# Retention's second transposes written three half units behind the norm, and the first output weights asked for one unit sooner

## The chip, the core and the metric

The kernel runs on one core of a Trainium2 chip. The metric is the device time of one execution in microseconds (us); smaller is better. Of the core's engines these matter here: PE (TensorE: matmuls and transposes, with the weight loads PEld beside it), DVE (VectorE), ACT (ScalarE), POOL (GpSimd), and SP, whose queue issues nearly all transfers. Each engine takes its instructions in the order of its own list; between engines semaphores hold an instruction until what it needs is done.

## The reference, cut to what matters

Two batches of 512 rows and 1024 columns go through one layer. From the normed and modulated rows `h` one projection gives the inputs of two groups of heads: windowed attention (8 heads of 64) and retention (4 heads of 128, with a norm of each head's output and a gate). Their outputs stand side by side in `mix`, go through the output weights, and a gated residual add and an MLP follow.

```python
proj = h @ w_in[l]
q_a, k_a, v_a, q_r, k_r, v_r, g_r = jnp.split(proj, IN_OFFSETS, axis=-1)
o_a = windowed_attention(...)
o_r = bidirectional_retention(q_r, k_r, v_r, g_r, ...)
...
mu = jnp.mean(y, axis=-1, keepdims=True)          # the norm of one retention head
yc = y - mu
yn = yc * lax.rsqrt(jnp.mean(yc * yc, axis=-1, keepdims=True) + EPS)
return jax.nn.silu(g) * yn.reshape(B, S, RET_WIDTH)
...
x = x + g1 * (concatenate([o_a, o_r]) @ w_out[l])
```

## The kernel before

Every matrix product takes float32 operands as two parts, a rounded high part and the rest as a low part, and adds three products (high by high, high by low, low by high). So a weight block that arrives as `raw` (128 by 1024) is cast on ACT (`wh`, line 93), and DVE subtracts to get `wl` (line 101). The `raw` tiles have three buffers; on batch 1 the kept low parts of weights lie in the same three. A block that is used for both batches is written back to memory in its two parts (`kept`) and loaded from there the second time.

The work is written as **units**: one block of projection weights with its matmuls, in two half units. `run_units` loads the next unit's weights, then writes the present one's matmuls, and after each half unit it calls `between`, which moves the **stages** on by one step: generators for the attention blocks and the retention heads, which write a piece of their own work and then say with `yield n` how many half units are to pass until the next piece. So the matmuls of the units cover the chains of the stages. A scheduler then orders the instructions of each engine from priorities that follow the written order, and may move an instruction a good way if its operands are late. `hooks` are calls after a unit of a given number.

A retention head (`ret_head`, from line 405) goes: scores `prs` for four key blocks; each is scaled by the decay table `dtab` (`rsf`, DVE, line 416), cast (`rsc`, ACT, line 418) and its low part subtracted (DVE, line 419); the values go into `py`. `ryt` is `py` copied from the bank by ACT (line 436), and four transposes write `pyn` (line 440), so that rows lie on partitions. For each, DVE takes statistics (`bn`, `mv`, lines 444 and 445) and then `rva` (447); POOL raises it to the power -1/2 (`rrs`, 449); DVE makes the bias `rnb` (452); and ACT writes the normed tile `ryn` in four pieces (454). Four second transposes write `pyb` (line 459), and DVE multiplies by the gate into `mix` (460). Between `ryn` and `pyb` stands the `yield` that the change touches.

The four heads of batch 0 run while batch 1's projections `k`, `v`, `q` are written, and their ends reach into its attention. Batch 1's heads run while the projections `rq`, `rk` and `rg` of the later heads are written, and the last two end among the output units of batch 0 (`out_units(0)`). Such a unit multiplies the parts `ms` of a piece of `mix` (ACT line 760, DVE line 761) by a block `wo` of output weights into four banks `po` (lines 131, 132, 134). Background work, the modulation sums `jka_b` on DVE (line 178, one 1.28 us operation for half a loaded block), is filled in all along.

Banks: three for the units (`mm`), five for all else (`aux`): `py`, `prs`, `pyn`, `pyb`, the attention's `psc`, `ppt` and `po`, and the fourth bank of an output unit.

Of the kernel before, what the change touches and what calls it, by code (L numbers as in the profile page):

```python
# [24 lines left out]
RH, RHD = 4, 128  # L25
# [7 lines left out]
def trunk_kernel(ctx, tc, x0, x1, x0_t, x1_t, params, gate2_bias, w_ada_first, w_ada_t, w_ada_gate2, w_in_first, w_in,  # L33
# [19 lines left out]
    def aux_bank(name):  # L53
        return psum.tile([P, 512], F32, tag="aux", name=name, bufs=5)
# [4 lines left out]
    def r4f(name):  # L59
        return r4(name, F32).rearrange("p a n -> p (a n)")  # L60
# [10 lines left out]
    def f(ap):  # L71
        return ap.bitcast(F32)
# [13 lines left out]
    def raw_unit(src, name, spare=False):  # L86
        t = r4f(f"raw_{name}") if spare else work.tile([P, 1024], F32, tag="raw", name=f"raw_{name}", bufs=3)
        nc.sync.dma_start(t[:, :src.shape[1]], src)
        return t

    def split_high(t, name):
        w = [work.tile([P, 1024], F32R, tag="ws", name=f"w{s}_{name}", bufs=4) for s in "hl"]
        nc.scalar.copy(w[0], t)
        return w

    def split_unit(src, name, n):
        return split_raw(raw_unit(src, name), name, n)

    def split_raw(t, name, n):
        w = split_high(t, name)  # L100
        nc.vector.tensor_sub(w[1], t, f(w[0]))
        return [x.rearrange("p (a n) -> p a n", n=n) for x in w]
# [301 lines left out]
    def ret_head(b, h, q_, k_, v_, sg, mix):  # L404
        nm = f"{b}_{h}"
        dtab = decay_table(b, h)
        py = aux_bank(f"py_{nm}")
        sc = [None] * NT

        def scores(sb):  # L410
            ssl = slice(sb * P, (sb + 1) * P)
            psc = aux_bank(f"prs_{nm}_{sb}")
            mm3(psc, (k_[:, 0, ssl], k_[:, 1, ssl]), (q_[:, 0, :], q_[:, 1, :]), True, True)
            sf = f2(f"rsf_{nm}_{sb}")
            o = 384 - sb * P
            nc.vector.scalar_tensor_tensor(sf, psc, RHD ** -0.5, dtab[:, o:o + 512], ALU.mult, ALU.mult)
            sc[sb] = r4(f"rsc_{nm}_{sb}")
            nc.scalar.copy(sc[sb][:, 0, :], sf)
            nc.vector.tensor_sub(sc[sb][:, 1, :], sf, f(sc[sb][:, 0, :]))

        def values(sb):
            hsl = slice(h * P, (h + 1) * P)
            mm3(py, (v_[sb][:, 0, hsl], v_[sb][:, 1, hsl]), (sc[sb][:, 0, :], sc[sb][:, 1, :]), sb == 0, sb == NT - 1)

        scores(0)
        yield 1
        scores(1)
        yield 2
        for sb in range(NT):
            values(sb)  # L430
            if sb + 2 < NT:
                scores(sb + 2)
            if sb < NT - 1:
                yield 1
        yt = f2(f"ryt_{nm}")
        nc.scalar.copy(yt, py)
        yield 1
        pn = aux_bank(f"pyn_{nm}")
        for t in range(NT):
            nc.tensor.transpose(pn[:, t * P:(t + 1) * P], yt[:, t * P:(t + 1) * P], ident)  # L440
        mv = small([P, NT, 2], f"mv_{nm}")
        for t in range(NT):
            st = small([P, 6], f"bn_{nm}_{t}")
            nc.vector.bn_stats(st, pn[:, t * P:(t + 1) * P])
            nc.vector.bn_aggr(mv[:, t, :], st)
        va = small([P, NT], f"rva_{nm}")
        nc.vector.tensor_scalar(va, mv[:, :, 1], EPS, None, ALU.add)
        rs = small([P, NT], f"rrs_{nm}")
        nc.gpsimd.tensor_tensor(rs, va, neghalf[:, :NT], ALU.pow)
        yn = f2(f"ryn_{nm}")  # L450
        nb = small([P, NT], f"rnb_{nm}")
        nc.vector.scalar_tensor_tensor(nb, mv[:, :, 0], -1.0, rs, ALU.mult, ALU.mult)
        for t in range(NT):
            nc.scalar.activation(yn[:, t * P:(t + 1) * P], pn[:, t * P:(t + 1) * P], AF.Identity, bias=nb[:, t:t + 1],
                                 scale=rs[:, t:t + 1])
        yield 2
        pb = aux_bank(f"pyb_{nm}")
        for t in range(NT):
            nc.tensor.transpose(pb[:, t * P:(t + 1) * P], yn[:, t * P:(t + 1) * P], ident)
        nc.vector.scalar_tensor_tensor(mix[2 + h // 2][:, h % 2, :], pb, 0.5, sg, ALU.mult, ALU.mult)  # L460
# [61 lines left out]
    def decay_table(b, h):  # L522
        if b == 1:
            dt = mwork.tile([P, TW], F32, tag="dtab", name=f"dtab_{b}_{h}", bufs=2)
            nc.sync.dma_start(dt, kept_tables[h])
            return dt
        dt = mwork.tile([P, TW], F32, tag="dtab", name=f"dtab_{b}_{h}", bufs=2)

        nc.scalar.activation(dt, dl, AF.Copy, scale=lg[:, 0, h:h + 1])
        nc.vector.scalar_tensor_tensor(dt, dl, nlb[:, h:h + 1], dt, ALU.mult, ALU.min)  # L530
        nc.scalar.activation(dt, dt, AF.Exp)
        nc.sync.dma_start(kept_tables[h], dt)
        return dt
# [63 lines left out]
    def run_units(units, rate, hooks={}, pace=0.7):  # L597
        clock[3] = pace
        nxt = units[0].load()
        for n, u in enumerate(units):  # L600
            cur, nxt = nxt, (units[n + 1].load() if n + 1 < len(units) else None)
            if u.keep is not None:
                u.keep(cur)
            for _ in u.use(cur):
                between(rate)
            if n in hooks:
                hooks[n]()
# [53 lines left out]
    one = {}  # L661
# [48 lines left out]
    def out_units(b, late=None):  # L710
# [35 lines left out]
        def unit(hf, kq):  # L746
            hs = slice(hf * 512, (hf + 1) * 512)

            key = f"wo{hf}_{kq}"

            def load():
                if b == 1:
                    w = kept_unit(key, f"wo{b}_{hf}_{kq}", 512, (late, "ws2", 3))
                else:
                    w = split_unit(w_out[hf, kq], f"wo{b}_{hf}_{kq}", 512)
                if hf == 0:
                    ms = halves[kq] = []
                    for k in range(2):
                        m_ = r4(f"ms_{b}_{kq}_{k}")
                        nc.scalar.copy(m_[:, 0, :], mix[kq][:, k, :])  # L760
                        nc.vector.tensor_sub(m_[:, 1, :], mix[kq][:, k, :], f(m_[:, 0, :]))
                        ms.append(m_)
                if kq == 2:
                    gr[hf] = gate_row(0, b, hs)
                return w, halves[kq]

            def use(wm):
                w, ms = wm
                if kq == 0:
                    banks[hf] = [(mm_bank if t < 3 else aux_bank)(f"po_{b}_{hf}_{t}") for t in range(NT)]  # L770
                for ts_ in ((0,), (1,), (2,), (3,)) if kq == 3 else ((0, 1), (2, 3)):
                    mm3_late([(banks[hf][t], [ms[k][:, i, t * P:(t + 1) * P] for i in range(2)],
                               (w[0][:, k, :], w[1][:, k, :]), kq + k == 0, kq + k == 4) for t in ts_ for k in range(2)], 1)
                    if ts_[-1] == 1:
                        yield
                if kq == 3:
                    for t in range(NT):
                        if hf == 0:
                            x2[t] = x2_tile(t)
                            tc.keep_in_program_order(nc.sync.dma_start(x2[t], xin[b][t * P:(t + 1) * P, :]))  # L780
                        g_ = f2(f"go_{b}_{hf}_{t}")
                        nc.vector.tensor_tensor(g_, banks[hf][t], gr[hf], ALU.mult)
                        nc.vector.tensor_tensor(x2[t][:, hs], x2[t][:, hs], g_, ALU.add)
                        if hf == 1 and b == 1:
                            store(t)
                            squares(hf, t)
                            if t > 0:
                                scaled(t - 1)
                    if hf == 0:
                        later.append((clock[0] + 2, lambda: [squares(hf, t) for t in range(NT)]))  # L790
                    elif b == 1:
                        scaled(NT - 1)
                yield
            return Unit(load, use, None, (lambda wm: keep_unit(key, wm[0])) if b == 0 else None)

        def norm2():
# [399 lines left out]
    units = first_v  # L1196
    for h in range(RH):
        units = units + ret_units(hT[0], 0, h)
    run_units(units, 1.3, {7: lambda: extra.append(norm_x1())})
    units = attn_units(hT[1], 1) + ret_v_units(hT[1], 1)  # L1200
    for h in range(RH):
        units += ret_units(hT[1], 1, h)
    run_units(units, 1.3)
    units, norm2_0 = out_units(0)
    run_units(units, 1.0)
    flush()
# [5 lines left out]
    units, norm2_1 = out_units(1, late)  # L1212
# [367 lines left out]
```

## Time and profile before

| what | value |
|---|---|
| median of 3 runs | 1106.5 us (1105.95 to 1106.68) |
| the profiled execution | 1105.71 us, its span 1103.9 us |
| mean granted clock of TensorE | 0.998 |
| busy share of the span: PE, PEld, DVE, ACT, POOL | 98%, 81%, 78%, 47%, 4% |
| 196 to 247 us (51.0): PE busy, DVE busy | 48.48, 40.90 us |
| 364 to 378 us (14.0): PE busy, DVE busy | 12.87, 9.85 us |

A line of the profile in order of time gives the start, the time taken, the engine, the line of the kernel and the operation, the tile written and those read (without buffer numbers), and in brackets how long the engine stood before it and for whom. A matmul's time overlaps that of the next, so for PE the distance from start to start is what counts: 0.227 us for 512 columns. A list of waits gives the waiting engine with its tile, the one waited for, the sum in us, the number of times and the longest.

### The profile page before, as it was taken

The page shows a single profiled execution, that of the slowest core. Times are in us where ns is not written, and L with a number is a line of the kernel's source. Part 1 is how long each engine was busy: PE and PEld are TensorE (multiplying, and loading weights), DVE is VectorE, ACT ScalarE, POOL GpSimd, SP SyncE. Part 2 cuts the span into 40 slices and gives each one's busy share as a digit, 9 for nine tenths or more (in the row PEclk, how much of TensorE's full clock was granted, in tenths as well). Part 3 has the DMA queues.
Part 4 walks back from the last instruction along what each step waited for, and adds up shares of the span by engine and source line. Part 5 has one row for each costly group of instructions (what it writes and reads, how often), then busy time and mean ns, then how long its engine had stood idle before and what let it go on. Part 6 is the DMA issues. An engine that isn't in the chain of part 4 may idle for free.

```text
span 1103.9 us, 14022 instructions
## 1 busy us (share of the span) xinstructions
PE 1078.9 (98%) x5021; PEld 888.9 (81%) x5021; DVE 864.6 (78%) x1448; ACT 515.9 (47%) x885; POOL 49.0 (4%) x55
## 2 busy tenths in 40 slices
PE   7999999999999999999999999999999999999997
PEld 5777788778888788888888888888788888888886
DVE  7979989877887787889878777886659754589786
ACT  6576666545653433574333343333443733335342
POOL 1000000000000001000000000000000000002213
PEclk9999999999999999999999999999999999999999
DMA  9889698765545698734546444452883556525504
GB/s 374 334 301 322 248 379 289 234 194 176 181 139 191 233 360 300 274 123 139 189 169 198 155 162 166 169 181 105 307 322 106 187 194 203 198 77 191 191 19 153
DMA packets 86746, 232.73 MB, mean 211 GB/s; under 512 B 8578, under 2 KB 20882, under 8 KB 86676
## 3 DMA queue, kind: packets, MB, share of 16 engines
q1 hardware_dynamic: 86084, 231.25, 60.2%
q8 instruction: 39, 0.64, 0.2%
q10 hardware_dynamic: 432, 0.57, 0.1%
q14 instruction: 31, 0.25, 0.1%
q0 software_dynamic: 160, 0.02, 0.0%
HBM read 160.75 MB, written 71.06 MB: 210 GB/s over the span
## 4 chain that ended last, share of the span: by engine, by line
PE 87%; DVE 8%; ACT 2%; DMA 1%; issue 1%; POOL 0%; POOLq 0%; ACTq 0%; DVEq 0%
PE x L1350 16%; PE px_None L933 15%; PE y L1350 12%; PE py_None L933 11%; PE po L132 3%; PE po L134 3%; PE po L131 3%; PE po L393 2%; PE ppt L386 2%; PE psc L360 1%; PE pj_rq L131 1%; PE pj_rq L132 1%; PE pj_rq L134 1%; PE pj_rg L134 1%; PE pj_rk L132 1%; PE pj_rk L131 1%
## 5 line engine op out<-in xcount | busy, mean ns | idle before, releaser
L1290 DVE TENSOR_TENSOR uc_l<-ur,uc_h 128x1024 fp32r<-128x1024 f32 x56 | 68.4, 1221 | 53.1 <-ACT uc_h L1290 36.0
L1350 PE MATMUL x<-wc_h,uc_h 128*128 128x512 f32 (+1 forms) x264 | 100.9, 383 | 0.7 <-ACT adacc L246 0.7
L1350 PE MATMUL x<-wc_l,uc_h 128*128 128x512 f32 (+1 forms) x264 | 101.0, 383 | 0.0
L1350 PE MATMUL x<-wc_h,uc_l 128*128 128x512 f32 (+1 forms) x264 | 101.0, 383 | 0.0
L1290 ACT CAST uc_h<-ur 128x1024 fp32r<-128x1024 f32 x56 | 58.9, 1051 | 77.3 <-PE x L1350 25.1
L1350 PE MATMUL y<-wc_h,uc_h 128*128 128x512 f32 x192 | 74.7, 389 | 0.0
L1350 PE MATMUL y<-wc_l,uc_h 128*128 128x512 f32 x192 | 74.7, 389 | 0.0
L1350 PE MATMUL y<-wc_h,uc_l 128*128 128x512 f32 x192 | 74.7, 389 | 0.0
L1290 ACT CAST wc_h<-w 128x1024 fp32r<-128x1024 f32 x48 | 50.5, 1051 | 48.1 <-PE x L1350 24.7
L1290 DVE TENSOR_TENSOR wc_l<-w,wc_h 128x1024 fp32r<-128x1024 f32 x48 | 58.6, 1220 | 17.6 <-ACT wc_h L1290 13.8
L1350 PEld LDWEIGHTS x<-wc_h,uc_h 128*128 128x128 f32 x264 | 49.6, 188 | 10.9 <-ACT adacc L246 1.2
L1350 PEld LDWEIGHTS x<-wc_h,uc_l 128*128 128x128 f32 x264 | 49.6, 188 | 9.8
L1350 PEld LDWEIGHTS x<-wc_l,uc_h 128*128 128x128 f32 x264 | 49.6, 188 | 9.6
L131 PE MATMUL po<-wh_wo,ms 128*128 128x512 f32 x128 | 50.2, 396 | 0.0
L132 PE MATMUL po<-wh_wo,ms 128*128 128x512 f32 x128 | 49.8, 392 | 0.1
L178 DVE CUSTOM_DVE_ANT_0 jka_b<-raw_adat,cb,cols 128x1024 bf16<-128x1024 f32 x38 | 48.2, 1279 | 0.1
L838 ACT CAST wc_s4h<-raw_w 128x1024 fp32r<-128x1024 f32 x16 | 16.8, 1052 | 63.1 <-PE px_None L933 54.1
L370 ACT ACTIVATE st<-st,negm 128x256 f32<-128x256 f32 (+1 forms) x64 | 35.2, 554 | 15.6 <-DVE negm L365 15.6
L1350 PEld LDWEIGHTS y<-wc_h,uc_l 128*128 128x128 f32 x192 | 36.0, 188 | 7.5
L1350 PEld LDWEIGHTS y<-wc_h,uc_h 128*128 128x128 f32 x192 | 36.0, 188 | 7.5
L1350 PEld LDWEIGHTS y<-wc_l,uc_h 128*128 128x128 f32 x192 | 36.0, 188 | 7.5
L933 PE MATMUL py_None<-hch,wc_a 128*128 128x512 f32 x120 | 39.7, 389 | 0.0
(378 smaller groups left out, 2954.8 us busy)
## 6 DMA issues: line engine op xcount, KB each, us to landing
ur<-spill SPq DMA_DIRECT2D x56, 512.0 KB, 4.5
raw_adat<-in_w_ada_t_dram SPq DMA_DIRECT2D x36, 512.0 KB, 6.9
raw_w<-in_w_mlp_dram SPq DMA_DIRECT2D x32, 512.0 KB, 3.5
spill<-s SPq DMA_DIRECT2D x64, 256.0 KB, 3.7
w<-in_w_mlp_dram SPq DMA_DIRECT2D x32, 512.0 KB, 5.2
spill<-u SPq DMA_DIRECT2D x48, 256.0 KB, 2.0
raw_ada<-in_w_ada_t_dram SPq DMA_DIRECT2D x12, 512.0 KB, 9.3
x<-in_x_dram SPq DMA_DIRECT2D x12, 512.0 KB, 7.2
```

What stands on the lines that cost most here:

```text
L131: nc.tensor.matmul(ps, lhs[0], rhs[0], start=start, stop=False)
L132: nc.tensor.matmul(ps, lhs[late], rhs[1 - late], start=False, stop=False)
L134: nc.tensor.matmul(ps, lhs[1 - late], rhs[late], start=False, stop=stop)
L178: nc.vector.tensor_tensor_reduce(junk(f"jka_{name}_{sec}_{kc}_{b}"), t, cb[:, b, :], 1.0, bcol[:, sec * KC + kc:sec * KC + kc + 1] if bias ...
L360: nc.tensor.matmul(psc[:, :w], qs[hh][:, isl], k_[:, s, j0 * P:j1 * P], start=(s == 0), stop=(s == 1))
L370: nc.scalar.activation(st[hh][:, :w], st[hh][:, :w], AF.Exp, bias=negm[:, hh:hh + 1], scale=0.125, accum_out=den[:, hh:hh + 1])
L386: nc.tensor.transpose(pt[:, hh * P:(hh + 1) * P], st[hh][:, jj * P:(jj + 1) * P], ident)
L393: nc.tensor.matmul(po, va[:, j0 + jj, g].rearrange("p s e -> p (s e)"), pts[jj][:, s, :], start=(jj == 0 and s == 0), stop=(jj == nj - 1 a ...
L838: nc.scalar.copy(hi, src)
L933: self.last = nc.tensor.matmul(bank[:, cs], x[:, k, :], y, start=first and k == 0 and i == 0, stop=last and k == 3 and i == 2, skip_group_ ...
L1290: last_split[:] = [nc.scalar.copy(hi, src), nc.vector.tensor_sub(lo, src, f(hi))]
L1350: nc.tensor.matmul(out, left[n][x][:, i, ts_], right[n][y][:, i, cs], start=first and i == 0 and k == 0, stop=end and i == 1 and k == 2, s ...
```

## The change

Two edits. The first writes the second transposes of all four heads of batch 0 and of heads 0 and 1 of batch 1 three half units behind the norm, not two; for heads 2 and 3 of batch 1 it stays two. The second asks for the raw block of the first output weights in a hook behind the unit `len(units) - 2` of the list before (the units of batch 1), and `out_units` takes it from there, where it had asked for it itself when its first unit was loaded.

```diff
@@ -453,7 +453,7 @@
         for t in range(NT):
             nc.scalar.activation(yn[:, t * P:(t + 1) * P], pn[:, t * P:(t + 1) * P], AF.Identity, bias=nb[:, t:t + 1],
                                  scale=rs[:, t:t + 1])
-        yield 2
+        yield 3 if b == 0 or h < RH - 2 else 2
         pb = aux_bank(f"pyb_{nm}")
         for t in range(NT):
             nc.tensor.transpose(pb[:, t * P:(t + 1) * P], yn[:, t * P:(t + 1) * P], ident)
@@ -752,7 +752,8 @@
                 if b == 1:
                     w = kept_unit(key, f"wo{b}_{hf}_{kq}", 512, (late, "ws2", 3))
                 else:
-                    w = split_unit(w_out[hf, kq], f"wo{b}_{hf}_{kq}", 512)
+                    t = one.pop((key, b), None) or raw_unit(w_out[hf, kq], f"wo{b}_{hf}_{kq}")
+                    w = split_raw(t, f"wo{b}_{hf}_{kq}", 512)
                 if hf == 0:
                     ms = halves[kq] = []
                     for k in range(2):
@@ -1200,7 +1201,7 @@
     units = attn_units(hT[1], 1) + ret_v_units(hT[1], 1)
     for h in range(RH):
         units += ret_units(hT[1], 1, h)
-    run_units(units, 1.3)
+    run_units(units, 1.3, {len(units) - 2: lambda: one.update({("wo0_0", 0): raw_unit(w_out[0, 0], "wo0_0_0")})})
     units, norm2_0 = out_units(0)
     run_units(units, 1.0)
     flush()
```

How the built lists differ at the places that the prediction speaks of. In these rows the number after the operation's tile is the head (`py_2`), the head and key block (`prs_2_1`, `rsc_2_1`), or for `po_0_3` the half and the row block; the last number only tells buffers apart; `x4` is four in a row.

PE, where batch 0's output units begin, behind the second transposes of batch 1's head 1. Before:

```order
L459 MATMUL pyb_1_3861<-ident,ryn_1_3799 128x128 x4
L124 MATMUL py_2_3808<-rsc_2_0_3815,rv_0_2861 128x512
L125 MATMUL py_2_3808<-rsc_2_0_3815,rv_0_2861 128x512
L126 MATMUL py_2_3808<-rsc_2_0_3815,rv_0_2861 128x512
L124 MATMUL prs_2_2_3917<-rq_2_3527,rk_2_3598 128x512
L125 MATMUL prs_2_2_3917<-rq_2_3527,rk_2_3598 128x512
L126 MATMUL prs_2_2_3917<-rq_2_3527,rk_2_3598 128x512
L124 MATMUL py_2_3808<-rsc_2_1_3839,rv_1_2870 128x512
L131 MATMUL po_0_0_3898<-wh_wo_0_0_3873,ms_0_0_3877 128x512
```

Now:

```order
L459 MATMUL pyb_1_3908<-ident,ryn_1_3799 128x128 x4
L124 MATMUL prs_3_0_3917<-rq_3_3722,rk_3_3774 128x512
L125 MATMUL prs_3_0_3917<-rq_3_3722,rk_3_3774 128x512
L126 MATMUL prs_3_0_3917<-rq_3_3722,rk_3_3774 128x512
L131 MATMUL po_0_0_3892<-wh_wo_0_0_3867,ms_0_0_3871 128x512
L131 MATMUL po_0_1_3893<-wh_wo_0_0_3867,ms_0_0_3871 128x512
L131 MATMUL po_0_2_3894<-wh_wo_0_0_3867,ms_0_0_3871 128x512
L131 MATMUL po_0_3_3895<-wh_wo_0_0_3867,ms_0_0_3871 128x512
L124 MATMUL py_2_3825<-rsc_2_0_3832,rv_0_2847 128x512
```

Head 3's first scores have come up behind `pyb_1`; the first `po` stands four matmuls nearer to it, and head 2's `py` and second half of scores behind the `po`.

DVE at the same place, from head 1's `rnb` to the low parts `ms`. Before:

```order
L452 SCALAR_TENSOR_TENSOR rnb_1_3800<-mv_1_3782,rrs_1_3797 128x4
L416 SCALAR_TENSOR_TENSOR rsf_2_0_3813<-prs_2_0_3809,dtab_2_3806 128x512
L419 TENSOR_TENSOR rsc_2_0_3815<-rsf_2_0_3813,rsc_2_0_3815 128x512
L178 ISA jka_b_2_1_3831,mod_s_90<-raw_adat_3648,cb,cols 128x1024
L178 ISA mod_s_90 128x1
L416 SCALAR_TENSOR_TENSOR rsf_2_1_3837<-prs_2_1_3833,dtab_2_3806 128x512
L344 SCALAR_TENSOR_TENSOR rg_3_3854<-rg_3_3854,pj_rg_3_3818 128x512
L178 ISA jka_b_3_0_3859,mod_s_90<-raw_adat_3753,cb,cols 128x1024
```

Now:

```order
L452 SCALAR_TENSOR_TENSOR rnb_1_3800<-mv_1_3782,rrs_1_3797 128x4
L178 ISA jka_b_2_1_3821,mod_s_90<-raw_adat_3648,cb,cols 128x1024
L178 ISA mod_s_90 128x1
L416 SCALAR_TENSOR_TENSOR rsf_2_0_3830<-prs_2_0_3826,dtab_2_3823 128x512
L419 TENSOR_TENSOR rsc_2_0_3832<-rsf_2_0_3830,rsc_2_0_3832 128x512
L101 TENSOR_TENSOR wl_wo_0_1_3880<-raw_wo_0_1_3877,wh_wo_0_1_3879 128x1024
L344 SCALAR_TENSOR_TENSOR rg_3_3847<-rg_3_3847,pj_rg_3_3808 128x512
L178 ISA jka_b_3_0_3852,mod_s_90<-raw_adat_3747,cb,cols 128x1024
L178 ISA mod_s_90 128x1
L416 SCALAR_TENSOR_TENSOR rsf_2_1_3858<-prs_2_1_3854,dtab_2_3823 128x512
```

The second `rsf` of head 2 has gone behind the low half of the second output weights, the gate and one more `jka_b`.

The queue of transfers, round the first output weights. Before:

```order
L119 DMA wl_rg_3_3738<-kept_in_2037 128x1024
L525 DMA dtab_3_4079<-kept_t_101 128x896
L88 DMA raw_wo_0_0_3871<-in_w_out_dram 128x1024
L88 DMA raw_adat_3753<-in_w_ada_t_dram 128x1024
L110 DMA kept_wo_0_3895<-wh_wo_0_0_3873 128x1024
L88 DMA raw_wo_0_1_3883<-in_w_out_dram 128x1024
```

Now:

```order
L119 DMA wl_rg_3_3732<-kept_in_2037 128x1024
L525 DMA dtab_3_3914<-kept_t_101 128x896
L88 DMA raw_wo_0_0_3806<-in_w_out_dram 128x1024
L88 DMA raw_adat_3747<-in_w_ada_t_dram 128x1024
L110 DMA kept_wo_0_3889<-wh_wo_0_0_3867 128x1024
L88 DMA raw_wo_0_1_3877<-in_w_out_dram 128x1024
```

Nothing has changed place on this queue; the load of `raw_wo_0_0` still waits for a buffer that the last matmuls of the projection `rq` of head 3 free.

Of batch 0's heads: in PE's list `pyb` of head 1 stands at row 795 and that of head 2 at row 901 in both, with `pyn` of head 1 six matmuls earlier now; between `pyn` and `pyb` of head 3 stand 15 rows before and 43 now, the added ones being projection matmuls and the first attention block's transposes and values.

## The prediction

> **What bounds the kernel now.** I read the page first, then the list of waits on the matrix engine, then the lines in order of time round each wait.
>
> ```profile
> span 1103.9 us, 14022 instructions
> PE 1078.9 (98%) x5021; PEld 888.9 (81%) x5021; DVE 864.6 (78%) x1448; ACT 515.9 (47%) x885; POOL 49.0 (4%) x55
> ```
>
> PE is busy in 98% of the span, so only time in which PE stands still can be won, and every new wait of PE adds to the end. Over 182 to 490 us, the stretch from the retention of batch 0 to the first output units, the list of PE's waits is short:
>
> ```profile
> PE pyb L459 <- ACT ryn L454: 2.5, 2, 1.3
> PE px L268 <- ACT x L742: 1.5, 1, 1.5
> PE py L124 <- ACT rsc L418: 1.0, 1, 1.0
> ```
>
> The `pyb` waits are what the first edit speaks of: the second transposes come before the normed tile `ryn` is there. The `py` wait stands in the first output unit, which the second edit speaks of; `px` comes later and keeps its cause. To price a stall I take the time from one matmul's start to the next and subtract 0.227 us, the step of 512-column matmuls back to back. Head 1, head 2 and head 3 of batch 0, in order of time:
>
> ```profile
> 200.42 0.17 DVE L447 TENSOR_SCALAR rva<-mv 128x4 f32<-128x4 f32 x1
> 200.73 1.01 POOL L449 TENSOR_TENSOR rrs<-rva,neghalf 128x4 f32<-128x4 f32 x1 [18.78 <-DVE rva L447]
> 200.97 0.39 PE L131 MATMUL pj_v<-h,wh_v 128*128 128x512 f32 x1
> 201.77 0.16 DVE L452 SCALAR_TENSOR_TENSOR rnb<-mv,rrs 128x4 f32<-128x4 f32 x1 [1.18 <-POOL rrs L449]
> 201.97 1.16 ACT L454 ACTIVATE ryn<-pyn,rnb,rrs 128x128 f32<-128x128 f32 x3 [2.28 <-DVE rnb L452]
> 202.48 0.33 PE L459 MATMUL pyb<-ident,ryn 128*128 128x128 f32 x1 [1.12 <-ACT ryn L454]
> ...
> 224.28 0.17 DVE L447 TENSOR_SCALAR rva<-mv 128x4 f32<-128x4 f32 x1
> 225.20 1.28 DVE L178 CUSTOM_DVE_ANT_0 jka_b<-raw_adat,cb,cols 128x1024 bf16<-128x1024 f32 x1
> 226.41 0.16 DVE L452 SCALAR_TENSOR_TENSOR rnb<-mv,rrs 128x4 f32<-128x4 f32 x1
> 226.67 1.51 ACT L454 ACTIVATE ryn<-pyn,rnb,rrs 128x128 f32<-128x128 f32 x4 [2.49 <-DVE rnb L452]
> 226.73 0.39 PE L134 MATMUL pj_q<-h,wl_q 128*128 128x512 f32 x1
> 227.18 0.33 PE L459 MATMUL pyb<-ident,ryn 128*128 128x128 f32 x1
> 227.27 0.48 PE L124 MATMUL prs<-rq,rk 128*128 128x512 f32 x1
> 227.59 0.27 PE L459 MATMUL pyb<-ident,ryn 128*128 128x128 f32 x1
> ...
> 242.89 0.39 PE L131 MATMUL pj_rv<-wh_rv,h 128*128 128x512 f32 x1
> 244.62 0.30 PE L459 MATMUL pyb<-ident,ryn 128*128 128x128 f32 x1 [1.34 <-ACT ryn L454]
> ```
>
> Head 1 loses 202.48 - 200.97 - 0.227 = 1.28 us, head 2 227.18 - 226.73 - 0.227 = 0.22, head 3 244.62 - 242.89 - 0.227 = 1.50: together 3.0 us. The chain in front is `pyn`, four statistics on DVE, `rva`, the power on POOL (1.01 us), `rnb`, then four `ryn` that start 0.35 us apart. A matmul that follows a lone transpose takes 227.59 - 227.27 = 0.32 us to the next start, 0.09 more than the usual step; the four transposes of heads 2 and 3 stand scattered among matmuls, which costs about 3 x 0.09 more for each of the two heads than one block would, 0.5 us together.
>
> The place where the output units begin, batch 1's head 1 (`rnb`, `ryn`), head 2 (`rsf`, `rsc`, `py`) and the first unit's `ms` and `po`:
>
> ```profile
> 357.23 0.33 SPq L88 DMA_DIRECT2D raw_wo<-in_w_out_dram  x1
> 361.20 1.05 ACT L93 CAST wh_wo<-raw_wo 128x1024 fp32r<-128x1024 f32 x1 [3.38 <-DMA raw_wo<-in_w_out_dram]
> 362.28 1.22 DVE L101 TENSOR_TENSOR wl_wo<-raw_wo,wh_wo 128x1024 fp32r<-128x1024 f32 x1 [0.91 <-ACT wh_wo L93]
> 363.53 0.33 SPq L88 DMA_DIRECT2D raw_wo<-in_w_out_dram  x1
> 367.43 0.16 DVE L452 SCALAR_TENSOR_TENSOR rnb<-mv,rrs 128x4 f32<-128x4 f32 x1 [1.12 <-POOL rrs L449]
> 367.94 1.05 ACT L93 CAST wh_wo<-raw_wo 128x1024 fp32r<-128x1024 f32 x1 [3.53 <-DMA raw_wo<-in_w_out_dram]
> 368.90 1.50 ACT L454 ACTIVATE ryn<-pyn,rnb,rrs 128x128 f32<-128x128 f32 x4
> 370.94 0.69 DVE L419 TENSOR_TENSOR rsc<-rsf,rsc 128x512 fp32r<-128x512 f32 x1 [2.73 <-ACT rsc L418]
> 371.28 0.48 PE L124 MATMUL py<-rsc,rv 128*128 128x512 f32 x1
> 371.54 1.28 DVE L178 CUSTOM_DVE_ANT_0 jka_b<-raw_adat,cb,cols 128x1024 bf16<-128x1024 f32 x1
> 372.75 0.69 DVE L416 SCALAR_TENSOR_TENSOR rsf<-prs,dtab 128x512 f32<-128x512 f32 x1
> 373.47 0.62 ACT L418 CAST rsc<-rsf 128x512 fp32r<-128x512 f32 x1 [1.15 <-DVE rsf L416]
> 373.99 2.18 ACT L760 CAST ms<-mix 128x512 fp32r<-128x512 f32 x4
> 374.14 0.50 PE L124 MATMUL py<-rsc,rv 128*128 128x512 f32 x1 [1.03 <-ACT rsc L418]
> 374.66 1.19 PE L131 MATMUL po<-wh_wo,ms 128*128 128x512 f32 x4
> 377.09 0.51 PE L132 MATMUL po<-wh_wo,ms 128*128 128x512 f32 x1
> ```
>
> The weights' first cast waits 3.38 us for its load, the second 3.53; ACT takes its work in order, so `ryn` and `rsc` of the retention queue behind it, DVE then stands 2.73 us, and PE pays at the end: from 371.28 to 377.09 it goes 16 matmuls further, which is 16 x 0.227 = 3.6 us of work in 5.8 us, thus 2.2 us of stalls.
>
> **The change part by part.** It adds and removes no arithmetic. Both edits alter only when code is written out, and the built order says how far that carries.
>
> *The second transposes, heads of batch 0.* Head 1: `pyb` stays at row 795 of PE's list; `pyn` comes 6 matmuls sooner (6 x 0.227 = 1.4 us), but the table operation of head 3, which stood ahead of the chain on DVE, now stands inside it:
>
> ```profile
> L530 DVE SCALAR_TENSOR_TENSOR dtab<-dl,nlb,dtab x4: 1143/1146/1147, 51.4 to 194.1; 128x896 f32<-128x896 f32 x4
> ```
>
> 1.4 sooner less 1.15 for it leaves about 0.2: the stall goes from 1.28 to 1.1. Head 2: `pyb` stays at row 901, now as one block of four, so that all four `ryn` are needed. On DVE a `qs` and a `jka_b` (0.7 + 1.2) stand among its statistics where `rsc` and `qs` (0.6 + 0.7) stood, so `rva` comes about 0.6 later, at 224.85, but no `jka_b` stands ahead of `rnb` any more: by head 1's steps (0.31 and 1.04) `rnb` is there at 226.2, not 226.41. The first `ryn` follows 0.2 later, the fourth starts 3 x 0.35 behind that and ends after another 0.45, at 227.9; PE wants the fourth transpose at 226.73 + 0.227 + 3 x 0.11 = 227.29. That is 0.6 lost, and 0.25 more because `rsc` of head 3 now queues behind the block of `ryn`: 0.85 against 0.22. Head 3: between `pyn` and `pyb` stand 43 rows instead of 15, so its 1.50 goes. In exchange the first attention block's scores come earlier; following DVE and ACT through them, PE waits about 0.2 for the fourth `ryn` (a score takes the bank of `pyn`) and 0.3 for `mix` behind two `jka_b`. After: 1.1 + 0.85 + 0.5 = 2.45; before 3.0, and the 0.5 of scattered transposes. **About -1.0 us**; bounds -3.5 (no wait left at all, 3.0 + 0.5) and +1 (head 2 and the new waits twice as long, and head 1 as before).
>
> *Heads of batch 1, first output unit.* No `pyb` of batch 1 shows a wait, so there is nothing to win by holding them back; but head 3's scores move from some 95 instructions behind to just behind head 1's `pyb`, and DVE's order changes. From `rnb` (367.43): `jka_b` comes first (to 368.7), then `rsf` (to 369.3), `rsc`, and then, ahead of head 2's second `rsf`, the low half `wl_wo` of the second weights (1.22), the gate `rg` (0.6) and the next `jka_b` (1.2). The first weights are requested when the last matmul of `rq` for head 3 has freed a buffer; in the new order three matmuls of `py` stand behind that one instead of ahead, so each weight step is 0.7 sooner, the second cast at 367.26, `rsc` on DVE at 370.25. Then 370.25 + 0.6 + 1.14 + 0.6 + 1.2 = 373.8 for that `rsf`, against 372.75: 1.05 later. The casts `ms` stand behind its `rsc` on ACT, so PE's first `po` can start at 375.7, where it was 374.66. PE now has only head 3's three score matmuls (371.3 to 372.05) to run in front of it and waits 3.6 us. The low parts of `ms` then come in time. Against 2.2 before: **+1.4 us**. Bounds: -0.5 (`wl_wo` and `rg` find DVE idle after all, 1.9 us sooner) and +3.5 (a later landing, below).
>
> *The weights asked for sooner.* In the transfer queue's list nothing changes place: head 3's table load at row 183, `raw_wo` at 184, a background load, and the second `raw_wo` at 187, in both. Worth 0 by itself, apart from the 0.7 above; what would hide a longer landing is nothing, since ACT waits there already.
>
> *Later.* Heads 2 and 3 now share the output units. Following the same chain for head 3: `pyb` has 24 matmuls (5.5 us) behind `pyn`, the chain on DVE carries three extra `ms` differences (0.6 each), about 0.2 us of wait. **+0.2**, 0 to 1.
>
> Sum: 1105.7 (the profiled execution: span 1103.9 and 1.8 around it) - 1.0 + 1.4 + 0.2 = 1106.3. The median shown, 1106.5, is 0.8 above that execution, so I forecast **1107.1**.
>
> The transfer deserves a check against the Trainium skill. From issue (363.53) to the cast (367.94) the second weights took 4.4 us. "DMA: Bandwidth & Descriptors" (the section with the two cost components) gives about 2.0 us fixed plus bytes over 436 GB/s, so 3.2 us for these 512 KB, as an estimate; the trace disagrees. By the page, `ryn` would be set by `rnb`, the chain would run 0.5 sooner, and the sum would be 0.5 lower; the row decides here.
>
> **The rivals.** *The waits simply vanish* (chance 0.22). For it: head 3's cover grows to nearly three times its length, and `pyn` of head 1 comes 1.4 us sooner. Against it: heads 1 and 2 get no more matmuls between. Price: the 3.0 and the 0.5 won and nothing lost in the first output unit, 1106.5 - 3.5 = 1103.0.
>
> *The second weights land late* (0.18), the slower side. The landing times of these loads:
>
> ```profile
> DMA to landing us min/median/max: 3.6/5.0/6.1
> ```
>
> Here the two took 4.0 (357.23 to 361.20) and 4.4 us to their casts, and the second is asked for only when `wl_wo` has read the first. At 6.1 the second slips by 1.7, both together by 3.8, and `ryn`, `rsc`, `wl_wo` and `ms` with them, since nothing is left for PE in front of `po`: 1108.8 to 1110.9, of which I take 1109.8. It decides once the two take 1.6 us longer in sum than here. For it: ACT already stands idle at both casts, so there is no slack. Against it: the queue's order round them is the same.
>
> *The clock drops* (0.05).
>
> ```profile
> PEclk9999999999999999999999999999999999999999
> ```
>
> The granted clock stays at 9 tenths or more in all slices, and PE's longest wait in this stretch is 1.5 us; one of 3.6 us would be new. If the matmuls behind it ran at half rate for as long as it lasted, half of 3.6 us would be lost: 1108.9. "TensorE: Matmul & The Clock Gate" of the Trainium skill (Part 1) says that the clock is halved after an idle window of about 3.4 us, and that the window runs freely, so that a wait of this size seldom fills one; no run here shows it yet.
>
> *The change does not do what it says* (0.10): the scheduler puts the work back, heads 1 and 2 as shown, and all is as before, 1106.5.
>
> **How the numbers follow.** The forecast, waits traded one for another, has 0.45; of it 0.07 lies above 1108.7 and 0.03 below 1104.3. A difference under 0.2% (2.2 us) cannot be told from none in this kernel. Faster: 0.22 + 0.03 = 0.25. Slower: 0.18 + 0.07 and half of the 0.05, less a little for landings that are only somewhat late, 0.25. Same: the rest, 0.50. The forecast's own range is 1105.0 to 1109.0; to leave out no more than two tenths it reaches to 1103.3 and 1109.8.
>
> **What would show it.** Right: no wait at head 3's `pyb` in batch 0 and still about one at head 1's; four `pyb` of head 2 in one block behind a wait; in the first output unit the wait at `po` for `ms` where it was at `py` for `rsc`, 3 us or more, with `wl_wo` ahead of the second `rsf` on DVE. Wrong: head 1's wait gone, or that `po` wait under 2 us (then faster); or PE waits for a `raw_wo` landing, or matmuls at twice 0.227 us (then slower).

## The result

The changed kernel took 1112.2 us (median of 6 runs, 1111.7 to 1112.6), the kernel before 1106.6 us in the same comparison (1105.9 to 1107.0): a ratio of 1.0053, with an interval of 1.0042 to 1.0063. So the change costs 5.6 us; the forecast was 1107.1 with a range up to 1109.8. One matmul wait of 4.7 us and a spell of halved clock behind it make most of it. The same order of instructions, built once more and timed again (below), cost 4.7 us, so the size is known to about 1 us.

### The profile after

The page of the changed kernel: span, PE's busy time, and the granted clock in 40 slices.

```profile
span 1110.4 us, 14018 instructions
PE 1082.3 (97%) x5021; PEld 891.5 (80%) x5021; DVE 866.0 (78%) x1448; ACT 515.9 (46%) x885; POOL 49.9 (4%) x55
PEclk9999999999999899999999999999999999999999
```

PE does the same 5021 matmuls and is *busy* for 3.4 us longer; one clock slice shows an 8. PE's waits from 182 to 490 us:

```profile
PE po L131 <- ACT ms L761: 4.7, 1, 4.7
PE pyb L459 <- ACT ryn L454: 0.9, 2, 0.7
PE py L934 <- ACT wc_a L839: 0.7, 1, 0.7
PE po L131 <- DVE go L783: 0.3, 1, 0.3
PE py L124 <- ACT rsc L418: 0.2, 1, 0.2
```

The `pyb` waits shrank from 2.5 to 0.9 us as meant, and the longest wait of the whole stretch is new: the first output matmul waits for `ms`. The wait for `wc_a` is the same in the kernel before (0.7 us), and the `px` wait has not gone: it is 1.6 us and now stands just behind 490 us. To see where the time came from, take places in PE's list up to which both kernels have done the same matmuls. Two of them, before:

```profile
360.23 0.39 PE L124 MATMUL py<-rsc,rv 128*128 128x512 f32 x1
...
395.18 0.39 PE L131 MATMUL po<-wh_wo,ms 128*128 128x512 f32 x1
```

and after:

```profile
360.54 0.48 PE L124 MATMUL py<-rsc,rv 128*128 128x512 f32 x1
...
400.60 0.48 PE L131 MATMUL po<-wh_wo,ms 128*128 128x512 f32 x1
```

Up to 360 us, thus over all of batch 0's heads, the change costs 360.54 - 360.23 = 0.3 us; over the stretch from there to 395 us, which holds the first output units, 400.60 - 395.18 - 0.3 = 5.1; over the rest 6.5 (the spans) - 5.4 = 1.1. The first output unit in order of time, after:

```profile
356.97 0.33 SPq L88 DMA_DIRECT2D raw_wo<-in_w_out_dram  x1
362.11 1.05 ACT L93 CAST wh_wo<-raw_wo 128x1024 fp32r<-128x1024 f32 x1 [4.54 <-DMA raw_adat<-in_w_ada_t_dram]
...
368.89 1.05 ACT L93 CAST wh_wo<-raw_wo 128x1024 fp32r<-128x1024 f32 x1 [4.03 <-DMA raw_wo<-in_w_out_dram]
369.85 1.49 ACT L454 ACTIVATE ryn<-pyn,rnb,rrs 128x128 f32<-128x128 f32 x4
371.88 0.69 DVE L419 TENSOR_TENSOR rsc<-rsf,rsc 128x512 fp32r<-128x512 f32 x1 [2.04 <-ACT rsc L418]
372.25 0.40 PE L126 MATMUL prs<-rq,rk 128*128 128x512 f32 x1
372.49 1.22 DVE L101 TENSOR_TENSOR wl_wo<-raw_wo,wh_wo 128x1024 fp32r<-128x1024 f32 x1
373.63 0.68 DVE L344 SCALAR_TENSOR_TENSOR rg<-rg,pj_rg 128x512 f32<-128x512 f32 x1
374.23 1.28 DVE L178 CUSTOM_DVE_ANT_0 jka_b<-raw_adat,cb,cols 128x1024 bf16<-128x1024 f32 x1
375.43 0.68 DVE L416 SCALAR_TENSOR_TENSOR rsf<-prs,dtab 128x512 f32<-128x512 f32 x1
376.15 0.62 ACT L418 CAST rsc<-rsf 128x512 fp32r<-128x512 f32 x1 [3.80 <-DVE rsf L416]
376.67 2.17 ACT L761 CAST ms<-mix 128x512 fp32r<-128x512 f32 x4
377.34 2.08 PE L131 MATMUL po<-wh_wo,ms 128*128 128x512 f32 x4 [4.69 <-ACT ms L761]
```

The order on DVE is the one forecast: `wl_wo`, `rg`, `jka_b`, and only then head 2's second `rsf`, `rsc`, `ms`. It begins later than forecast: the first weights were requested 0.4 us later than reckoned and took 5.1 us from request to cast (before: 4.0), so the second cast came at 368.89 where 367.26 had been reckoned. (The profile puts the end of that first wait down to the background load requested 0.4 us behind the weights; in four other kernels with the same gap to the load ahead it names `raw_wo`, after 4.8 to 5.0 us.) PE goes 372.25 to 377.34 between two matmuls, 4.86 us more than a step of 0.227. And the four `po` then take 2.08 us, where they took 1.19. The same place by time stretches (the number ahead of the last two is the granted clock):

```profile
375.00:376.00 1.00, 0.00 (x0) 0.00 (x0) 1.00 (x3) 0.00 (x0) 0.00 (x0) 0.80 1.04 426
376.00:377.00 1.00, 0.00 (x0) 0.00 (x0) 1.00 (x3) 0.85 (x2) 0.00 (x0) 0.50 1.04 410
...
381.00:382.00 1.00, 1.00 (x4) 0.81 (x3) 1.00 (x1) 0.00 (x0) 0.00 (x0) 0.50 0.00 0
382.00:383.00 1.00, 1.00 (x5) 0.79 (x5) 0.12 (x2) 0.00 (x0) 0.00 (x0) 0.79 0.00 0
```

The clock is at half from 375.6 to 382.4. PE works from 377.34, so by estimate half of 382.4 - 377.34 is lost, 2.5 us. Together: 4.86 - 2.2 (the stalls before) + 2.5 = 5.2, against 5.1 by the fixed places.

### The profile page after: what moved, and what is told of

It is laid out like the page before. It is cut to its first block, busy times and chain, and to the rows that moved or that the text cites. A ratio compares the mean times of both kernels' runs of the same rounds, so it can differ in the third digit from the quotient of the medians.

```text
span 1110.4 us, 14018 instructions
## 1 busy us (share of the span) xinstructions
PE 1082.3 (97%) x5021; PEld 891.5 (80%) x5021; DVE 866.0 (78%) x1448; ACT 515.9 (46%) x885; POOL 49.9 (4%) x55
## 4 chain that ended last, share of the span: by engine, by line
PE 86%; DVE 9%; ACT 2%; issue 1%; DMA 1%; POOL 1%; POOLq 0%; DVEq 0%; ACTq 0%
PE x L1351 16%; PE px_None L934 15%; PE y L1351 12%; PE py_None L934 11%; PE po L131 3%; PE po L132 2%; PE po L134 2%; PE po L393 2%; PE ppt L386 2%; PE psc L360 2%; DVE jka_b L178 1%; PE pj_rq L131 1%; PE pj_rq L132 1%; PE pj_rq L134 1%; PE pj_rk L132 1%; PE pj_rk L131 1%
```

## The experiments

All times are medians, beside a median of the kernel before on the same chip.

### Which edit, and which heads

**Batch 0's heads alone.**

```diff
-        yield 2
+        yield 3 if b == 0 else 2
```

> Later second transposes for the four heads of batch 0 alone; batch 1's heads and the weight request as before. Theory A (the longer last heads of batch 0 push every later stage on by half a unit, so that in batch 1 head 3's scores fall in front of the first output unit): PE waits about 4.7 us at the first output matmul for the first ms, the matmuls behind it run at half clock, 1111 to 1112.5 us. Rival B (as the prediction put it: the heads of batch 1 that are held back make the new order): no such wait, about 1106.8 us (batch 0's own balance, +0.3).

Measured: 1110.9 us (before 1106.0), ratio 1.0047 [1.0032, 1.0062], 0.1 us under the range expected. The longest of its waits of PE:

```profile
PE po L131 <- ACT ms L760: 4.8, 1, 4.8
```

Theory A holds: batch 0's heads alone make the wait in batch 1.

**Batch 1's heads 0 and 1 alone.**

```diff
-        yield 2
+        yield 3 if b == 1 and h < RH - 2 else 2
```

> Later second transposes for heads 0 and 1 of batch 1 alone. Theory A: the first output unit stays as before, no wait over 2 us at its first matmul, 1106 to 1107 us. Rival B: the 4.7 us wait and the half clock are here, 1111 us or more.

Measured: 1105.6 us (before 1106.0), ratio 0.9995 [0.9986, 1.0005]. Its three longest waits are those of before:

```profile
PE pyb L459 <- ACT ryn L454: 2.5, 2, 1.3
PE px L268 <- ACT x L742: 1.4, 1, 1.4
PE py L124 <- ACT rsc L418: 0.9, 1, 0.9
```

Rival B, which is how the prediction told it, falls: the edited heads of batch 1 do neither harm nor good.

**One head: head 3 of batch 0.**

```diff
-        yield 2
+        yield 3 if b == 0 and h == 3 else 2
```

> The later second transposes for one head alone, head 3 of batch 0. Theory A (one half unit more at the end of batch 0's stages is enough to shift all later stages): the wait at the first output matmul stands as in the whole change, 4 to 5 us, with the half clock behind it; the wait at head 3's transposes (1.34 us) is gone: 1110 to 1111.5 us. Rival B (the shift needs the heads of batch 1, or all four of batch 0): the gain alone, 1105 us.

Measured: 1111.0 us (before 1105.6), ratio 1.0052 [1.0035, 1.0069]; the two longest waits of PE:

```profile
PE po L131 <- ACT ms L760: 3.7, 1, 3.7
PE pyb L459 <- ACT ryn L454: 1.1, 1, 1.1
```

One half unit at the end of batch 0 costs as much as the whole change, though the wait is 3.7 us where 4 to 5 were expected; the clock was at half for 6.8 us here. The kernel keeps only two stages going at a time, so a head that ends later lets every later stage start later. PE's built order at the first output matmul, before, ends with head 2's own matmuls:

```
pyb_1 x4 | py_2 (rsc_2_0) x3 | prs_2_2 x3 | py_2 (rsc_2_1) x1 | po_0_0 ...
```

and with this one edit, 130 us after the edited place, it reads:

```
prs_2_1 x3 | pyb_1 x4 | prs_3_0 x3 | po_0_0 ...
```

Head 2 is four of its `py` matmuls and a score block further back, and PE has only head 3's three `prs` in hand while the chain of head 2's `rsf` and `rsc`, which `ms` queues behind, is still open.

**The first edit without the sooner request.**

```diff
-    run_units(units, 1.3, {len(units) - 2: lambda: one.update({("wo0_0", 0): raw_unit(...)})})
+    run_units(units, 1.3)
```

> The first edit alone, for all six heads; the weights are asked for where the kernel before asks. On every engine and in the transfer queue the instructions stand in the same order as in the whole change, so theory A says: the same time as the whole change, 1111 to 1112.5 us. Rival (the sooner request does something by itself): 1 us or more away from that.

Measured: 1110.7 us (before 1106.1), ratio 1.0040 [1.0025, 1.0056]; that is 0.3 us under the range expected and overlaps the whole change's interval. The orders are the same instruction for instruction on PE, DVE, ScalarE and the transfer queue, so the second edit changes nothing.

### The late landing

**First try: spare tiles, requested one unit sooner.**

```diff
-    {len(units) - 2: lambda: one.update({("wo0_0", 0): raw_unit(w_out[0, 0], "wo0_0_0")})}
+    {len(units) - 3: lambda: one.update({("wo0_0", 0): raw_unit(w_out[0, 0], "wo0_0_0", True),
+                                         ("wo0_1", 0): raw_unit(w_out[0, 1], "wo0_0_1", True)})}
```

> The changed kernel with the first two output weights loaded into spare tiles one unit sooner, so that neither cast waits for a load; PE's and DVE's orders are the same. Theory A (order and late loads add up): ryn and rsc of head 2 start about 1.5 us sooner, the wait at the first output matmul falls from 4.7 to about 3.2 us; 1110.7 us if the clock still drops, 1108.3 us if it stays. Rival (the order on DVE alone makes the wait, loads don't matter): 1112.2 us.

Measured: 1110.3 us (before 1106.0), ratio 1.0043 [1.0026, 1.0060]; the wait at `po` is 4.6 us. The trace says why this decides nothing:

```profile
354.56 0.32 SPq L525 DMA_DIRECT2D dtab<-kept_t  x1
356.19 1.28 SPq L88 DMA_DIRECT2D raw_wo<-in_w_out_dram  x3
...
362.54 1.05 ACT L93 CAST wh_wo<-raw_wo 128x1024 fp32r<-128x1024 f32 x1 [1.17 <-DMA raw_wo<-in_w_out_dram]
```

The requests stood behind the decay table in the transfer queue, left together, and the first took 6.3 us to its cast: no sooner than before. The second cast, at 363.81 in this trace, no longer stood in front of `ryn`, but the late first one held `wl_wo` on DVE, and head 1's statistics behind it.

**Second try: requested ahead of the decay table.**

```diff
-    {len(units) - 3: ...
+    {len(units) - 5: ...
```

> The changed kernel with the first two output weights in spare tiles and asked for ahead of head 3's decay table in the transfer queue, so that they land before ScalarE comes to their casts. PE's order is the same; on DVE the second weights' low half and two statistics stand a few places earlier. If late landings made the part of the wait that was not forecast (4.9 where 3.6 us were): the second cast no longer stands in front of ryn, rsc of head 2 is ready at 370.5, the wait at the first output matmul falls to 3.4 to 3.7 us and the first output matmul starts 1.2 us sooner. Rival (DVE's order sets the wait, and something else takes the place of the landings): the wait stays at 4.5 us or more. In either case it stays over 3 us, since rg and jka_b still stand ahead of rsf; time 1109 to 1111 us.

Measured: 1110.2 us (7 runs, 1108.3 to 1111.7; before 1106.3), ratio 1.0035 [1.0023, 1.0047]. ScalarE and PE in order of time:

```profile
351.13 1.05 ACT L93 CAST wh_wo<-raw_wo 128x1024 fp32r<-128x1024 f32 x1 [3.16 <-DMA raw_wo<-in_w_out_dram]
...
363.71 1.05 ACT L93 CAST wh_wo<-raw_wo 128x1024 fp32r<-128x1024 f32 x1 [0.26 <-PE pj_rk L132]
...
368.50 1.51 ACT L454 ACTIVATE ryn<-pyn,rnb,rrs 128x128 f32<-128x128 f32 x4 [3.26 <-DVE rnb L452]
376.37 2.07 PE L131 MATMUL po<-wh_wo,ms 128*128 128x512 f32 x4 [3.37 <-ACT ms L761]
```

The first cast still waits for its load, but 11 us sooner than in the changed kernel; the second, at 363.71, waits for none, and `ryn` starts right behind `rnb`. The wait is 3.4 us, at the lower end of the 3.4 to 3.7 expected. So the late landing made some 1.3 of the 4.7 us, and what stays is the chain on DVE (`wl_wo`, `rg` and `jka_b` still run ahead of the second `rsf`). The time is 3.9 us above the kernel before, where the change cost 4.7 to 5.6; that is about what the shorter wait gives, but the intervals overlap. In this execution the clock was still halved (375.0 to 381.8). Of the seven runs of this one program, two had a mean granted clock of 0.998 and took 1108.3 and 1108.5 us; those at 0.995 took 1110.2 to 1111.7.

### The halved clock

Idle matmuls behind head 3's first `prs`, into a bank that is overwritten later; n = 11, 13 and 6. With 11 and 6 the order of everything else is unchanged; with 13 five rows of PE's list behind the first output matmuls change place.

```diff
             mm3(psc, (k_[:, 0, ssl], k_[:, 1, ssl]), (q_[:, 0, :], q_[:, 1, :]), True, True)
+            if (b, h, sb) == (1, 3, 0):
+                for _ in range(n):
+                    nc.tensor.matmul(py, k_[:, 0, ssl], q_[:, 0, :], start=True, stop=True, ...)
```

> The changed kernel with 11 idle matmuls (11 x 0.227 = 2.5 us, into a bank that is overwritten) between head 3's scores and the first output matmul, where PE waits 4.7 us; the order of all else is the same. If the half clock behind the wait is due to PE's standing still: the wait shrinks to about 2.2 us, the granted clock stays at 1.00 from 372 to 384, and the time falls by the 2.5 us that the slow matmuls cost, to 1109.7 us. Rival (the clock drops for another reason, such as the time or the work behind): the idle matmuls hide in the wait, nothing changes, 1112.2 us.

Measured with 11: 1109.9 us (10 runs, 1107.4 to 1113.8; before 1106.0), ratio 1.0039 [1.0028, 1.0050]. Its median is the expected one, and its mechanism is not:

```profile
376.00:378.00 2.00, 0.79 (x3) 0.67 (x4) 2.00 (x4) 1.98 (x4) 0.00 (x0) 1.00 0.90 365
378.00:380.00 2.00, 2.00 (x6) 1.51 (x5) 2.00 (x4) 1.25 (x3) 0.00 (x0) 0.54 0.05 12
380.00:382.00 2.00, 2.00 (x7) 1.59 (x6) 2.00 (x4) 0.00 (x0) 0.00 (x0) 0.61 0.00 0
```

The wait was 1.92 us, and the clock still went to half, from 378.2 to 381.6, beginning 0.9 us *after* PE had started again. So a short wait can be enough, and it isn't its length alone that counts. That gave theory C, which the next two were to test.

> As with 11 idle matmuls, but 13, so that about 1.5 us of standing still is left in front of the first output matmul. Theory C (the clock is judged in windows of 3.41 us that run freely, and halved for the next window when PE was busy in less than about half of one): 1.5 us can leave no window under 55% busy, so the clock is never halved there; every run at 1110 us or less, median about 1108.7 us, and a spread like that of the kernel before (2.7 us). Rival (any wait of over about 1.4 us can halve it, or the cause is not PE's standing still): runs up to 1112 us or more, as with 11.

Measured with 13: 1110.9 us (5 runs, 1109.6 to 1112.4; before 1106.1), ratio 1.0044 [1.0031, 1.0056].

```profile
377.16 1.20 PE L131 MATMUL po<-wh_wo,ms 128*128 128x512 f32 x4 [1.51 <-ACT ms L764]
...
378.00:380.00 2.00, 2.00 (x10) 1.60 (x9) 2.00 (x4) 1.20 (x3) 0.00 (x0) 1.00 0.04 10
380.00:382.00 2.00, 2.00 (x10) 1.62 (x10) 1.95 (x4) 0.00 (x0) 0.00 (x0) 1.00 0.00 0
...
398.11 0.48 PE L131 MATMUL po<-wh_wo,ms 128*128 128x512 f32 x1
```

In the profiled execution the clock stayed at 1.00. The place that the changed kernel reached at 400.60 comes at 398.11 here, 2.5 us sooner (the idle matmuls left out of the count); the first output matmul began 0.2 us sooner, so the halved clock had cost about 2.3 us there. But the expectation on the runs fails, and they look as the rival has it: of the other four one took 1109.8 us with a mean clock of 0.998, three took 1110.9 to 1112.4 with 0.995 or 0.996. Where the clock fell in those, whether the wait was longer or another one did it, stays open, since only one execution was profiled; the `px` wait near 489 us, 2.2 us in that one, is a candidate.

> As with 11 idle matmuls, but 6, so that about 3.3 us of standing still is left. Theory C: wherever the windows of 3.41 us fall, one of them has over 1.65 us of it, so the clock is always halved for one or two windows: median about 1110.8 us, no run under 1109 us. Rival (only a wait longer than a whole window of 3.4 us halves it): the clock stays, 1109 us or less.

Measured with 6: 1110.2 us (4 runs, 1108.5 to 1111.3; before 1106.1), ratio 1.0036 [1.0023, 1.0050]; wait 3.0 us, clock at half from 377.1 to 380.5. That speaks against the rival in the profiled execution; one run of 1108.5 us at a clock of 0.998 lies under the bound of theory C, so "always" is not borne out.

### The wait taken away

`ms` is split from batch 0's `mix`, which is complete long before. Splitting it four units sooner takes it out of the queue behind `rsc`:

```diff
-                if hf == 0:
-                    ms = halves[kq] = [] ...   # the two splits
+                if hf == 0 and kq not in halves:
+                    split_mix(kq)
...
+    units_0, norm2_0 = out_units(0)
+    run_units(units, 1.3, {..., len(units) - 4: lambda: [norm2_0.split_mix(q) for q in (0,)]})
```

On the changed kernel:

> The changed kernel with the first unit's two ms split four units sooner (their source, batch 0's mix, is complete long before), so that the first output matmuls wait neither for rsf and rsc of head 2 nor for the weights. If the queue of ms behind rsc on ScalarE is what sets the wait: no wait over 1.5 us between 370 and 385, granted clock 1.00, 4.9 + 2.5 us less: 1105 us. Rival (PE then only waits at the next thing, head 2's py or the second unit's ms): a wait of 3 us or more there, 1109 us or more.

Measured: 1104.4 us (before 1105.6), ratio 0.9987 [0.9978, 0.9996].

```profile
PE px L268 <- ACT x L750: 1.3, 1, 1.3
...
372.00:377.00 5.00, 5.00 (x25) 4.13 (x24) 4.91 (x8) 1.20 (x3) 0.00 (x0) 1.00 0.97 359
```

The wait is gone (the longest that is left in this stretch is the `px` wait), PE is busy without a break from 372 to 377, the clock stays, and nothing takes the wait's place. So the wait for `ms`, with the halved clock behind it, is what the change lost. Two further kernels have the sooner split without the change, and with batch 0's part alone:

> The kernel before with the first unit's two ms split four units sooner. Theory A: of its 2.2 us of stalls round the first output unit most goes, 1104 to 1104.5 us. Rival (the stalls move on to the second unit): 1106 us.

Measured: 1104.1 us (before 1105.6), ratio 0.9986 [0.9976, 0.9995].

> Later second transposes for batch 0's four heads together with the first unit's ms split four units sooner. Theory A (all the loss sits at the first output unit): 1110.9 - 4.9 - about 1.8 of half clock = 1104.2 us, so it would be faster than the kernel before by what batch 0 and that unit gave. Rival (the new order has other costs behind the first unit, some 1 us by the trace of the changed kernel): 1105.5 us.

Measured: 1104.6 us (before 1105.6), ratio 0.9991 [0.9981, 1.0000], nearer to theory A's 1104.2 than to the rival's 1105.5.

With the first output unit out of the way, the kernel is as fast without the change (1104.1) as with it (1104.4): no gain of the later transposes by themselves shows. The last kernel keeps them only at head 3 of batch 0:

> The later second transposes for head 3 of batch 0 alone, with the first unit's ms split four units sooner. Theory A (the first output unit took all of the loss, and head 3's own wait of 1.3 us is won, less 0.6 to 0.8 us of new small waits in the next projection): 1103.5 us, 0.5 us under the kernel before with the same split. Rival (that gain is eaten by the later stages): 1104.1 us or more.

Measured: 1103.8 us (before 1106.1), ratio 0.9979 [0.9970, 0.9988], the lowest of all. From its waits of PE:

```profile
PE pyb L459 <- ACT ryn L454: 1.1, 1, 1.1
...
PE pj_rv L131 <- DVE mx L362: 0.6, 1, 0.6
...
PE ppt L386 <- ACT st L378: 0.2, 1, 0.2
```

Head 3's wait is gone and 0.8 us of small ones have come for it in the next projection, as expected (and 0.3 us at `go`, as in the changed kernel); the interval overlaps that of the split alone, so the head's own share isn't told apart.

## Why the prediction was wrong

**The sign of the whole was right, its size was not.** The prediction saw waits traded for others and took -1.0, +1.4 and +0.2. The fixed places give +0.3, +5.1 and +1.1, so the first term, the gain, has the wrong sign, and that the sum came out on the right side is owed to the second.

**The term that failed most: "Heads of batch 1, first output unit", +1.4.** Its mechanism is in the trace as told: `wl_wo`, `rg` and `jka_b` ahead of the second `rsf`, and `po` waiting for `ms`. Three things were wrong with it.
- The wait was sized 3.6 us and measured 4.86. The working counted the first landing as the 4.0 us of before; it took 5.1, though the row of landings that the prediction shows has a median of 5.0. It also let the request come 0.7 us sooner; it came 0.3 sooner. With the landings out of the way the wait is 3.4 us: the chain on DVE was sized well, and the rest came from a transfer that had been named a rival. That rival was to decide from 1.6 us of extra landing on; 1.2 came, and counted in full all the same.
- The clock rival, chance 0.05 and 1.8 us, is nearly half of the loss: 2.3 to 2.5 us. The prediction had seen that a wait of 3.6 us would be new, and then let a rule on the clock make it unlikely. "TensorE: Matmul & The Clock Gate" of the Trainium skill (Part 1) says that the gate looks at windows of 3.41 us that run freely; the lengths here agree, 3.4 us in four executions and 6.8 (two windows) in four. It also speaks of an idle window, and there the traces differ: a window need not be idle to halve the clock.
- The cause was put down to batch 1's held-back heads. Batch 1's part alone gives 0.9995, head 3 of batch 0 alone 1.0052. That head 3's scores move to just behind head 1's `pyb` was true of the built order; the step was wrong about what moved them.

**"The second transposes, heads of batch 0", -1.0: +0.3.** 0.15 of this stood already at 13 us, ahead of any change. Head 1 and head 3 did about as told (from start to start 0.87 us lost at head 1, 0.7 of it in the list of waits, and none at head 3). Head 2 did not:

```profile
225.83 1.07 PE L134 MATMUL pj_q<-h,wl_q 128*128 128x512 f32 x4
226.58 1.50 ACT L454 ACTIVATE ryn<-pyn,rnb,rrs 128x128 f32<-128x128 f32 x4 [4.64 <-DVE rnb L452]
227.09 1.37 PE L459 MATMUL pyb<-ident,ryn 128*128 128x128 f32 x4 [0.19 <-ACT ryn L454]
228.64 0.50 PE L124 MATMUL py<-rsc,rv 128*128 128x512 f32 x1 [0.18 <-ACT rsc L418]
```

From the last `pj_q` (225.83 + 3 x 0.227 = 226.51) to `py` at 228.64 stand one matmul and four transposes, 0.67 us of work in 2.13: 1.46 lost, where 0.85 was reckoned. In one block the transposes run at ScalarE's pace, 0.35 us for each `ryn`, and this block hides nothing; the list of waits shows only 0.19 of it, since every piece is short. The new waits behind head 3 were sized 0.5. What is left over by the fixed places, with the prediction's 0.5 for the scattered transposes counted as won, is some 1.3 us for them; it is spread, with no single stop of PE over 0.3 us, and was not traced.

**"The weights asked for sooner", 0.** Right: nothing moves.

**"Later", +0.2.** 1.1 by the fixed places. Of it about 0.5 comes at a new wait for `go` behind the first four output units (the list has 0.3 of it); the rest is spread over the output units that follow, up to about 437 us of the kernel before, and not traced.

**The check of the transfer.** The rate and the fixed time that the prediction takes from "DMA: Bandwidth & Descriptors" of the Trainium skill are given there as a fit for transfers that POOL issues; SP issues these. The rows decide, and here they are 3.4 to 6.3 us.

**The other rivals.** "The waits simply vanish" failed at head 1 and at the output unit. "The change does not do what it says" failed: the orders of heads 2 and 3 of batch 0 and of the first output unit changed as told.

## What to carry over

A knob that lets one piece of work end later also moves everything that waits for its place: compare the built order a long way behind the edit, and test the pieces of an edit separately before telling which of them did it. Where PE's cover in front of a chain is down to a few matmuls, price the transfer in that chain at its usual and its slow time, not at the one seen, and a spell of half clock with the wait: it came with eight of the nine profiled waits at this place. A wait behind a queue of other work is often cheapest removed by writing its input earlier: here two splits moved four units ahead were worth more than the transposes.

## What was not expected of the hardware

**The clock is halved after the fact, for 3.4 us or twice that, and not only by a stretch without any work.** In the nine profiled executions with a wait of 1.5 to 4.8 us at this place, eight show the half clock there, for 3.4 us (four) or 6.8 us (four). With batch 0's edit alone PE stood still from 372.8 to 377.6 at a clock of 1.00 throughout, and the half clock came at 378.1, when it was working again. Take 3.41 us, the length of one spell, as a window, lay such windows end to end from the changes of clock, and count the matmul columns in each as a share of what fits in at full speed. The count is rough, to some 0.03, since a matmul's columns are placed by its start alone and transposes take longer than their columns say; the first 25 us, with other kinds of matmul, are left out. At full clock, it was halved after shares of 0 to 0.34, all at this place. It stayed after 0.31 and 0.34 here (one execution each), after 0.31 to 0.37 near 490 us in six executions (the `px` wait), and after all shares above. Already halved, it stayed so after 0.13 to 0.36 and came back after 0.49 and more. So a boundary near a third of full work is an estimate, and the count settles it no closer; the "about half" of theory C was too high. A wait of 1.9 us (11 idle matmuls) was enough when it fell into one window; with batch 0's edit alone the 4.8 us were shared by two windows, and only the second, at 0.10, was followed by half clock.

**A load that leaves soon after another lands later.** From request to cast the first output weights took 4.0 us when requested 2.3 us behind the decay table's load (the kernel before), 5.1 us at 1.6 us behind it (the changed kernel), and 6.3 us when two more loads left right behind it. The other profiled executions with the load at this place agree: 3.4 to 3.6 us in four with a gap of 2.0 to 2.3 us, 4.6 to 5.0 us in seven with a gap of 1.6 us. That the decay table's load itself is what delays them is not shown.
